# Attention scores taken from the longest block of queries to the shortest, weights normalised in pairs, and a head turned from its last keys to its first

## The chip, the cores and the metric

The kernel runs on one core of one Trainium2 chip. The metric is the device time of one execution in microseconds (us), as the median of several runs. TensorE (PE in the rows) multiplies matrices; VectorE (DVE), ScalarE (ACT) and GpSimd (POOL) work on tiles element by element; SyncE (SP) only issues transfers, and POOL issues some too.

## The reference, cut to what matters

Two layers stand behind each other, on 512 tokens of 1024 numbers. The change lies in layer 1, forgetting attention with 16 heads of 64:

```python
q, k, v, g, f = jnp.split(h @ w_in, [FOX_W, 2 * FOX_W, 3 * FOX_W, 4 * FOX_W], axis=-1)
q = _rms_norm(q.reshape(b, s, FOX_HEADS, FOX_HD), q_gain).transpose(0, 2, 1, 3) * (FOX_HD ** -0.5)
k = _rms_norm(k.reshape(b, s, FOX_HEADS, FOX_HD), k_gain).transpose(0, 2, 1, 3)
cum = jnp.cumsum(log_f, axis=1).transpose(0, 2, 1)
for qs in range(0, s, Q_BLOCK):                      # Q_BLOCK = 128: four blocks of queries
    qe = qs + Q_BLOCK
    logits = (jnp.einsum('bhqd,bhkd->bhqk', q[:, :, qs:qe], k[:, :, :qe])
              + cum[:, :, qs:qe, None] - cum[:, :, None, :qe])
    causal = jnp.arange(qs, qe)[:, None] >= jnp.arange(qe)[None, :]
    p = jax.nn.softmax(jnp.where(causal, logits, -jnp.inf), axis=-1)
    outs.append(jnp.einsum('bhqk,bhkd->bhqd', p, v[:, :, :qe]))
o = jnp.concatenate(outs, axis=2).transpose(0, 2, 1, 3).reshape(b, s, FOX_W)
return (o * jax.nn.silu(g)) @ w_out
```

Block `i` of queries sees `(i + 1) * 128` keys, so the four blocks of a head have 128, 256, 384 and 512 columns.

## The kernel before, in words

**Scheduling.** The program is recorded as tasks and then put in order, when it is built, by a list scheduler (`Sched.order`): a planner with its own costs keeps one queue for each engine and takes from it the ready task with the smallest due time (`prio`), if its buffers are free. The due time is the PE work recorded so far, less an offset. `merge` and `zip2` interleave generators, so that attention (the side) is due a little ahead of the projections (the main work). What comes out is one fixed order for each engine, and an engine that waits holds all that stands behind it. All instructions go through one helper, so the profile gives line 442 for nearly all of them, and they are told apart by their tiles.

**A head of attention.** `stacks(pair)` turns the normalised q and k of two heads (tile `qn`) and splits them into a high and a low part (`st`). `scores(head)` works on the four blocks: two matmuls into a PSUM bank `r` (`r<-st,st`, 128, 256, 384 or 512 columns), an addition of the bias `ck` with a running minimum on DVE (`lg<-r,ck`, the custom instruction, which also gives the row's minimum `mn`), and the exponential on ACT with its row sum (`lg<-lg,t` and a read of the accumulator). After the fourth block one reciprocal of the four sums (`t<-t`, 128x4) follows on DVE, and then POOL multiplies each block by its reciprocal (`TENSOR_SCALAR lg<-lg,t`), blocks 0, 1, 2, 3. `turn(head)` transposes the weights on PE (`r<-ident,lg`), for each block `j` of keys the blocks of queries `j` to 3, and splits the bank into a high part (ACT, `ph<-r`) and a low part (DVE, `ph<-r,ph`). `values(head)` multiplies them with v (`r<-ph,v`), `j` from 0 to 3, and adds the two halves into `oT`. In `heads`, `scores(h + 1)` runs interleaved with `turn(h)`, and then `values(h)` with `stacks` of a later pair.

**What runs beside it.** The projections of the second half of q, k, v (`p<-wh,big`, `p<-wl,big`) run beside heads 0 to 7, and those of the gate (`p<-big,wh`, `p<-big,wl`) beside heads 8 to 15. The rms norm of q and k is a chain of short DVE instructions on 128x16 tiles (`t<-t,t`, `t<-t`) that ends in two products `qn<-qn,t`. Weights come as `raw` and are split into `wh` (ACT) and `wl<-raw,wh` (DVE); the last ones are first multiplied by a gate (`raw<-raw,gate`, DVE). After the last exponential ACT takes the Silu of the gate (`qn<-qn`), DVE multiplies (`oT<-oT,qn`), both split it (`goh`), and the output projection (`a<-wh,goh`) starts.

**Buffers.** The blocks of one head lie in three buffers: blocks 0 and 2 share one, block 1 and block 3 have their own. There are four PSUM banks of kind `r`, shared by scores, turns, values and stacks.

Of the kernel before, what the change touches and what calls it, by code (L numbers as in the profile page):

```python
# [19 lines left out]
NT = S // P  # L20
# [501 lines left out]
def trunk(tc, x, c, positions, mod_w, mod_b, norm_g, ret_w_in, ret_w_out, fox_w_in, fox_b_f,  # L522
# [6 lines left out]
    with ExitStack() as es:  # L529
# [7 lines left out]
        V, A, G, T, SY = s.vector, s.scalar, s.gpsimd, s.tensor, s.sync  # L537
# [4 lines left out]
        def small(n=1):  # L542
            return s.buf("t", n)
# [4 lines left out]
        def pr_(n=512):  # L548
            return s.buf("r", n)
# [31 lines left out]
        def split(src, dst_h, dst_l, eng=None):  # L581
            A.copy(dst_h, src)
            (eng or V).tensor_tensor(out=dst_l, in0=src, in1=dst_h, op=ALU.subtract)
# [214 lines left out]
        for nm_ in ORD.split():  # L798
            if nm_[0] == "m":
                j, nj = int(nm_[1]), int(nm_[3])  # L800
# [354 lines left out]
        def blocks(kind, dt):  # L1155

            b = [s.buf(kind, 512, dt) for _ in range(5)]
            return [(b[0], b[1]), (b[2][:, 0:384], b[3][:, 0:384]), (b[4][:, 0:256], b[4][:, 256:512]),
                    (b[2][:, 384:512], b[3][:, 384:512])]
# [305 lines left out]
        stk, prob, ptr, last_exp = {}, {}, {}, [None]  # L1465

        def scores(head):

            q, k, kx = stk.pop(head)
            ck = s.buf("ck", 7 * P)  # L1470
            with s.at(-30.0):
                SY.dma_start(ck, cum_dram[head].partition_broadcast(P))
                G.dma_start(ck[:, 2 * P:3 * P], k_mask[:, 0:P], accum_op=ALU.add)
                G.dma_start(ck[:, 4 * P:7 * P], k_mask, accum_op=ALU.add)
            cks = [ck[:, 6 * P:], ck.rearrange("p (k n) -> p k n", k=7, n=P)[:, 0:6:5, :], ck[:, 0:3 * P],
                   ck[:, 0:6 * P].rearrange("p (k n) -> p k n", k=2, n=3 * P)[:, :, 0:2 * P]]
            b = [s.buf("lg") for _ in range(3)]
            lg = [b[0][:, 384:512], b[2][:, 0:256], b[0][:, 0:384], b[1]]
            mn, sm, rs = small(NT), small(NT), small(NT)
            for i in range(NT):  # L1480
                n = (i + 1) * P
                ps = pr_()
                cs = slice(i * P, n)
                T.matmul(ps[:, 0:n], q[:, cs], k[:, 0:n], start=True, stop=False)
                T.matmul(ps[:, 0:n], q[:, cs], kx[:, 0:n], start=False, stop=True)

                def two(v):
                    return v.rearrange("p (k n) -> p k n", k=2, n=n // 2) if i % 2 else v

                V.tensor_tensor_reduce(out=two(lg[i]), in0=two(ps[:, 0:n]), in1=cks[i], scale=1.0, scalar=3.0e38,  # L1490
                                       op0=ALU.add, op1=ALU.min, accum_out=mn[:, i:i + 1])
                last_exp[0] = A.activation(lg[i], lg[i], AF.Exp, bias=mn[:, i:i + 1], scale=-1.0,
                                           accum_out=sm[:, i:i + 1])
                if i == NT - 1:
                    V.reciprocal(rs, sm)
                    for j in range(NT):
                        G.tensor_scalar(out=lg[j], in0=lg[j], scalar1=rs[:, j:j + 1], scalar2=1.0,
                                        op0=ALU.mult, op1=ALU.mult)
                    prob[head] = lg
                yield max(2 * n, 512) / 512 * 0.216  # L1500

        def turn(head):

            parts = prob.pop(head)
            pt = ptr[head] = blocks("ph", F32R)
            for j in range(NT):
                w = S - j * P
                ps = pr_()
                for i in range(j, NT):
                    T.transpose(ps[:, (i - j) * P:(i - j + 1) * P], parts[i][:, j * P:(j + 1) * P], ident)  # L1510
                split(ps[:, 0:w], *pt[j])
                yield (NT - j) * 0.107
# [31 lines left out]
        def heads(lo, hi, nxt):  # L1544

            for h in range(lo, hi):
                if h + 1 < nxt:
                    yield from zip2(scores(h + 1), turn(h))
                else:
                    yield from turn(h)  # L1550
                if h % 2 == 1 and h // 2 + 2 < nxt // 2:
                    yield from zip2(stacks(h // 2 + 2), values(h))
                else:
                    yield from values(h)
# [33 lines left out]
        run(q0)  # L1588
        merge(proj1("k", 0), forget_gates(), 0.5, B1, s)
        merge(proj1("v", 0), chain(stacks(0), stacks(1), scores(0)), 0.3, B1, s)  # L1590
        merge(proj1("qkv", 1), heads(0, 8, 16), R1, B1, s)
        merge(chain(*[proj_g(j) for j in range(4)]), heads(8, 16, 16), R2, B1, s)
# [77 lines left out]
```

## Time and profile before

| | us |
|---|---|
| median of 3 runs | 731.32 |
| lowest, highest | 730.45, 733.33 |
| profiled execution, its own time | 731.09 |
| its span, first to last instruction | 729.3 |
| mean granted clock of TensorE, share of full speed | 0.992 |

The span is that of one execution, and its own time is 1.8 us above the span. Attention in layer 1 takes from about 480 us to 680 us of the span. Of a matmul the profile models the end, so a "busy" PE can hide a short wait; the spacing of two starts shows it. For DVE, ACT and POOL the row gives the duration, and in brackets the idle time ahead of the row and who ended it.

### The profile page before, as it was taken

To read this page: it belongs to the slowest core of one execution; us is meant where nothing else is said; L and a number is where in the kernel's file an instruction comes from. 1 tells how busy PE (TensorE), PEld (TensorE's weight loads), DVE (VectorE), ACT (ScalarE), POOL (GpSimd) and SP (SyncE) were. 2 spreads that over 40 slices of the span, in tenths; PEclk is the share of its full clock that TensorE was granted. 3 is DMA by queue.
4 is the path that set the end of the run, shared out by engine and by line. 5 is a ranking of instruction groups with operands and counts; after the bars stand their busy time and mean duration, and the time that the engine had idled before them with its cause. 6 is when DMAs were issued, how large, how long until landed. Compare 5 with 4: busy or idle time off the path is not lost.

```text
span 729.3 us, 10006 instructions
## 1 busy us (share of the span) xinstructions
PE 707.8 (97%) x3386; PEld 579.1 (79%) x3386; DVE 587.5 (81%) x1257; ACT 394.2 (54%) x733; POOL 118.9 (16%) x167
## 2 busy tenths in 40 slices
PE   7999999999999999999999999999999999998995
PEld 6777888888887888888888887787778688877884
DVE  5899999989996899899381869877688967788925
ACT  6558563654354435554150554447758566778613
POOL 1001100100110011000000100054343354444011
PEclk9999999999999999999999999999999999999998
DMA  8994764794757674625435127494545566667002
GB/s 281 348 310 95 176 210 131 201 269 135 174 142 200 192 172 140 175 91 200 131 121 185 74 75 256 145 233 112 152 106 138 147 152 152 130 156 260 1 11 104
DMA packets 78546, 118.25 MB, mean 162 GB/s; under 512 B 6952, under 2 KB 39840, under 8 KB 78496
## 3 DMA queue, kind: packets, MB, share of 16 engines
q1 hardware_dynamic: 66176, 98.71, 42.6%
q0 software_dynamic: 12320, 18.91, 14.7%
q8 instruction: 26, 0.43, 0.2%
q14 instruction: 24, 0.20, 0.1%
HBM read 109.16 MB, written 4.25 MB: 156 GB/s over the span
## 4 chain that ended last, share of the span: by engine, by line
PE 77%; DVE 10%; DMA 5%; issue 3%; ACT 2%; POOL 1%; SPq 1%; DVEq 0%; POOLq 0%; ACTq 0%
PE p L442 44%; PE a L442 18%; PE r L442 15%; DMA raw<-in_mod_w 4%; DVE wl L442 2%; DVE t L442 1%; DVE macc L442 1%; POOL lg L442 1%; DVE st L442 1%; DVE ph L442 1%; DVE sx L442 1%; SPq L442 1%; DVE tg L442 1%; DVE lg L442 1%; DMA raw<-in_fox_w_in 1%
## 5 line engine op out<-in xcount | busy, mean ns | idle before, releaser
L442 ACT CAST wh<-raw 128x1024 fp32r<-128x1024 f32 x120 | 124.8, 1052 | 80.9 <-PE p L442 40.8
L442 DVE TENSOR_TENSOR wl<-raw,wh 128x1024 fp32r<-128x1024 f32 x120 | 146.9, 1229 | 26.0 <-ACT wh L442 23.0
L442 PE MATMUL p<-wh,big 128*128 128x512 f32 x384 | 136.3, 403 | 0.0
L442 PEld LDWEIGHTS p<-wh,big 128*128 128x128 f32 x384 | 72.1, 189 | 13.3
L442 PE MATMUL p<-wh,sf 128*128 128x512 f32 x256 | 79.7, 390 | 0.0
L442 PE MATMUL p<-wl,big 128*128 128x512 f32 x192 | 76.8, 400 | 0.0
L442 PE MATMUL p<-wh,act 128*128 128x512 f32 x192 | 64.2, 396 | 1.2 <-DVE big L442 1.2
L442 POOL DMA_DIRECT2D raw<-in_ret_w_in x16 | 19.4, 1239 | 268.3 <-DVE raw L442 87.8
L442 DVE SCALAR_TENSOR_TENSOR macc<-raw,csilu,macc 128x512 f32<-128x512 f32 x80 | 59.7, 747 | 2.8 <-DMA raw<-in_mod_w 2.0
L442 PE MATMUL a<-wh,go 128*128 128x512 f32 x192 | 61.7, 392 | 0.0
L442 POOL TENSOR_SCALAR lg<-lg,t 128x128 f32<-128x128 f32 (+1 forms) x64 | 43.3, 759 | 80.0 <-DVE t L442 75.4
L442 PEld LDWEIGHTS p<-wh,sf 128*128 128x128 f32 x256 | 48.0, 188 | 10.3 <-ACT u L442 0.3
L442 PE MATMUL p<-act,wh 128*128 128x512 f32 x160 | 53.1, 393 | 0.0
L442 PE MATMUL p<-wl,sf 128*128 128x512 f32 x128 | 50.0, 391 | 0.0
L442 ACT ACTIVATE lg<-lg,t 128x128 f32<-128x128 f32 (+1 forms) x64 | 36.2, 566 | 19.3 <-DVE t L442 18.8
L442 PE MATMUL p<-big,wh 128*128 128x512 f32 x128 | 45.7, 415 | 0.0
L442 PEld LDWEIGHTS p<-wh,act 128*128 128x128 f32 x192 | 36.0, 188 | 8.4 <-issue 1.6
L442 PEld LDWEIGHTS a<-wh,go 128*128 128x128 f32 x192 | 36.0, 188 | 7.0
L442 PEld LDWEIGHTS p<-wl,big 128*128 128x128 f32 x192 | 36.2, 189 | 6.1
L442 PE MATMUL r<-act,sh 128*128 128x512 f32 x120 | 40.6, 391 | 0.0
L442 POOL DMA_DIRECT2D ck<-in_k_mask x32 | 28.6, 1047 | 69.2 <-DVE t L442 55.3
L442 PE MATMUL p<-wl,act 128*128 128x512 f32 x96 | 38.3, 398 | 0.6 <-DVE wl L442 0.6
(184 smaller groups left out, 1521.5 us busy)
## 6 DMA issues: line engine op xcount, KB each, us to landing
raw<-in_ret_w_in SPq DMA_DIRECT2D x48, 512.0 KB, 5.6
raw<-in_mod_w SPq DMA_DIRECT2D x64, 256.0 KB, 6.5
raw<-in_fox_w_in SPq DMA_DIRECT2D x32, 512.0 KB, 4.6
raw<-in_ret_w_in POOLq DMA_DIRECT2D x16, 512.0 KB, 8.8
raw<-in_mod_w SPq DMA_DIRECT2D x16, 512.0 KB, 4.6
raw<-in_ret_w_out SPq DMA_DIRECT2D x16, 512.0 KB, 4.2
ck<-cum_dram SPq DMA_DIRECT2D x16, 448.0 KB, 4.5
x<-in_x SPq DMA_DIRECT2D x16, 256.0 KB, 5.4
```

Source lines behind the costliest of these rows:

```text
L442: getattr(eng, op)(*[real(v) for v in args], **{k: real(v) for k, v in kw.items()})
```

## The change

The blocks of queries are taken from block 3 (512 columns) to block 0. A reciprocal is now taken for two blocks at a time, as soon as the second of the pair has its sum: for blocks 2 and 3, and then for blocks 1 and 0; POOL multiplies block 3, 2, 1, 0 in that order. `turn` goes from the last block of keys, which needs block 3 alone, to the first, which needs all four. `values` is unchanged and still begins with the first block of keys.

```diff
-            for i in range(NT):
+
+            for i in reversed(range(NT)):
                 n = (i + 1) * P
                 ps = pr_()
                 cs = slice(i * P, n)
@@
                 last_exp[0] = A.activation(lg[i], lg[i], AF.Exp, bias=mn[:, i:i + 1], scale=-1.0,
                                            accum_out=sm[:, i:i + 1])
-                if i == NT - 1:
-                    V.reciprocal(rs, sm)
-                    for j in range(NT):
+                if i % 2 == 0:
+                    V.reciprocal(rs[:, i:i + 2], sm[:, i:i + 2])
+                    for j in (i + 1, i):
                         G.tensor_scalar(out=lg[j], in0=lg[j], scalar1=rs[:, j:j + 1], scalar2=1.0,
                                         op0=ALU.mult, op1=ALU.mult)
-                    prob[head] = lg
+                prob[head] = lg
                 yield max(2 * n, 512) / 512 * 0.216
 
         def turn(head):
 
             parts = prob.pop(head)
             pt = ptr[head] = blocks("ph", F32R)
-            for j in range(NT):
+            for j in reversed(range(NT)):
                 w = S - j * P
                 ps = pr_()
                 for i in range(j, NT):
```

The planner's order moves with it from head 0 on. Three places show how.

**PE, the transposes of the last head (15).** Before: `lg_6637` holds blocks 0 and 2, `lg_6657` block 1, `lg_6694` block 3; the banks `r_6738`, `r_6755`, `r_6767`, `r_6780` take the blocks of keys 0 to 3.

```order
L442 MATMUL r_6738<-ident,lg_6637 128x128
L442 MATMUL r_6755<-ident,lg_6637 128x128
L442 MATMUL r_6767<-ident,lg_6637 128x128
L442 MATMUL p_6736<-big_3872,wh_6328 128x512
L442 MATMUL p_6736<-big_3880,wh_6328 128x512
L442 MATMUL p_6736<-big_3872,wl_6343 128x512
L442 MATMUL r_6738<-ident,lg_6694 128x128
L442 MATMUL r_6755<-ident,lg_6694 128x128
L442 MATMUL r_6767<-ident,lg_6694 128x128
L442 MATMUL r_6780<-ident,lg_6694 128x128
```

After, on PE at the same place: `lg_6638` is block 3, `lg_6658` holds blocks 2 and 0, `lg_6678` is block 1; `r_6728`, `r_6732`, `r_6741` take the blocks of keys 3, 2 and 1, and `r_6763`, four rows further on, block 0.

```order
L442 MATMUL r_6728<-ident,lg_6638 128x128
L442 MATMUL p_6548<-big_3889,wh_6274 128x512
L442 MATMUL r_6732<-ident,lg_6658 128x128
L442 MATMUL r_6732<-ident,lg_6638 128x128
L442 MATMUL p_6548<-big_3903,wh_6274 128x512
L442 MATMUL p_6548<-big_3889,wl_6287 128x512
L442 MATMUL r_6741<-ident,lg_6678 128x128
L442 MATMUL r_6741<-ident,lg_6658 128x128
L442 MATMUL r_6741<-ident,lg_6638 128x128
```

Before, the transposes follow the blocks of queries as they come, into up to four open banks, and all four that read block 3 stand at the end; after, a bank is filled in one go, and the first need only the block that is normalised first.

**PE, from the last turn but one to its values (head 14).** Before: the last transpose into the bank of key block 0 (`r_6648`), and the first matmul of the values (`r_6712<-ph_6696`), which reads it.

```order
L442 MATMUL r_6648<-ident,lg_6598 128x128
L442 MATMUL r_6664<-ident,lg_6598 128x128
L442 MATMUL r_6678<-ident,lg_6598 128x128
L442 MATMUL p_6670<-big_3872,wl_6343 128x512
L442 MATMUL p_6670<-big_3872,wh_6328 128x512
L442 MATMUL p_6670<-big_3880,wh_6328 128x512
L442 MATMUL p_6670<-big_3872,wl_6343 128x512
L442 MATMUL r_6700<-ident,lg_6598 128x128
L442 MATMUL p_6670<-big_3872,wh_6328 128x512
L442 MATMUL p_6670<-big_3880,wh_6328 128x512
L442 MATMUL p_6670<-big_3872,wl_6343 128x512
L442 MATMUL r_6712<-ph_6696,v_5865 128x512
```

After, on PE from the same transpose (now into `r_6689`) to the two matmuls that read the high part (`ph_6701`) and the low part (`ph_6708`) of key block 0:

```order
L442 MATMUL r_6689<-ident,lg_6550 128x128
L442 MATMUL p_6548<-big_3889,wl_6287 128x512
L442 MATMUL p_6548<-big_3889,wh_6274 128x512
L442 MATMUL p_6548<-big_3903,wh_6274 128x512
L442 MATMUL p_6548<-big_3889,wl_6287 128x512
L442 MATMUL r_6710<-ph_6701,v_5886 128x512
L442 MATMUL p_6548<-big_3889,wh_6274 128x512
L442 MATMUL p_6548<-big_3903,wh_6274 128x512
L442 MATMUL p_6548<-big_3889,wl_6287 128x512
L442 MATMUL r_6710<-ph_6708,v_5886 128x512
```

Seven 512-column matmuls and three transposes stood between the bank and the first matmul that reads it; now four matmuls stand there.

**DVE, the last rms norm of k.** Before: the chain on `t_5596` and `t_5599`, with the reciprocal of one head (`t_5601`) in it.

```order
L442 TENSOR_SCALAR t_5596<-t_5583 128x16
L442 TENSOR_TENSOR t_5599<-t_5596 128x16
L442 RECIPROCAL t_5601<-t_5490 128x4
L442 TENSOR_TENSOR t_5599<-t_5599,t_5583 128x16
L442 SCALAR_TENSOR_TENSOR t_5596<-t_5599,t_5596 128x16
L442 TENSOR_TENSOR t_5599<-t_5596 128x16
```

After, on DVE: the same chain is on `t_5614` and `t_5617`, and the last reciprocal ahead of it (`t_5534`) belongs to that head's blocks 1 and 0.

```order
L442 RECIPROCAL t_5534<-t_5495 128x2
L442 SCALAR_TENSOR_TENSOR t_5518<-t_5525,t_5518 128x16
L442 TENSOR_TENSOR qn_5451<-qn_5451,t_5518 128x512
L442 TENSOR_TENSOR qn_5477<-qn_5477,t_5518 128x512
L442 TENSOR_REDUCE t_5550<-tm_5563 128x8
L442 TENSOR_TENSOR ph_5596<-r_5539,ph_5572 128x512
L442 TENSOR_SCALAR t_5603<-t_5550 128x16
L442 TENSOR_TENSOR wl_5605<-raw_5461,wh_5579 128x1024
L442 TENSOR_SCALAR t_5614<-t_5603 128x16
L442 TENSOR_TENSOR t_5617<-t_5614 128x16
L442 TENSOR_TENSOR t_5617<-t_5617,t_5603 128x16
```

The reciprocals have moved out of the last chain into the one before it.

## Rows read from the trace of the kernel before

**Rows 1.** The page's first part: busy time of each engine, its share of the span, and its instructions.

```profile
PE 707.8 (97%) x3386; PEld 579.1 (79%) x3386; DVE 587.5 (81%) x1257; ACT 394.2 (54%) x733; POOL 118.9 (16%) x167
```

**Rows 2.** Busy time by stretch: the stretch in us from the span's start and its length, then busy us (and instructions) of PE, PEld, DVE, ACT, POOL, the granted clock, the DMA share and GB/s. The first is all of attention, the others are 20 us each in it.

```profile
480.00:680.00 200.00, 194.40 (x1012) 157.99 (x1011) 155.04 (x374) 140.35 (x317) 79.74 (x122) 1.00 0.61 150
520.00:540.00 20.00, 19.70 (x101) 15.70 (x101) 19.48 (x58) 16.41 (x38) 4.84 (x8) 1.00 0.54 132
560.00:580.00 20.00, 18.27 (x95) 14.10 (x94) 19.06 (x53) 12.03 (x27) 5.92 (x10) 1.00 0.58 146
640.00:660.00 20.00, 18.75 (x104) 15.49 (x103) 17.04 (x42) 14.17 (x35) 8.21 (x12) 1.00 0.54 133
660.00:680.00 20.00, 18.02 (x90) 14.56 (x89) 17.61 (x32) 17.36 (x34) 5.38 (x4) 1.00 0.67 235
```

**Rows 3.** Who waited for whom from 480 to 680 us, PE and its weight load (PEld): waiting engine and tile, releaser, then us in total, times, longest.

```profile
PE r L442 <- POOL lg L442: 3.3, 4, 1.8
PE r L442 <- DVE qn L442: 1.5, 1, 1.5
PEld r L442 <- POOL lg L442: 5.0, 5, 2.3
```

**Rows 4.** The timeline of PE at six places: start, us, instruction, and in brackets the idle time ahead of it. The last two rows are an undisturbed pair, the two before them an undisturbed run of four transposes and what follows.

```profile
496.46 0.40 PE L442 MATMUL p<-wl,big 128*128 128x512 f32 x1
497.13 0.33 PE L442 MATMUL r<-ident,lg 128*128 128x128 f32 x1 [0.27 <-POOL lg L442]
...
535.82 0.39 PE L442 MATMUL p<-wh,big 128*128 128x512 f32 x1
536.45 0.33 PE L442 MATMUL r<-ident,lg 128*128 128x128 f32 x1 [0.24 <-DVE ph L442]
...
571.32 0.40 PE L442 MATMUL p<-wl,big 128*128 128x512 f32 x1
573.23 0.33 PE L442 MATMUL r<-ident,qn 128*128 128x128 f32 x1 [1.52 <-DVE qn L442]
...
649.74 0.39 PE L442 MATMUL p<-big,wh 128*128 128x512 f32 x1
651.18 0.33 PE L442 MATMUL r<-ident,lg 128*128 128x128 f32 x1 [1.06 <-POOL lg L442]
...
664.42 0.44 PE L442 MATMUL p<-big,wh 128*128 128x512 f32 x1
665.02 0.33 PE L442 MATMUL r<-ident,lg 128*128 128x128 f32 x1 [0.16 <-POOL lg L442]
...
667.36 0.40 PE L442 MATMUL p<-big,wl 128*128 128x512 f32 x1
669.58 0.66 PE L442 MATMUL r<-ident,lg 128*128 128x128 f32 x4 [1.82 <-POOL lg L442]
669.99 0.71 PE L442 MATMUL p<-big,wh 128*128 128x512 f32 x2
...
677.32 0.39 PE L442 MATMUL p<-big,wl 128*128 128x512 f32 x1
677.55 0.39 PE L442 MATMUL a<-wh,goh 128*128 128x512 f32 x1
```

**Rows 5.** The timeline of POOL: the four normalisations of one head merged into a row (x4, all four widths), at three heads, and the widest block of the last head alone.

```profile
541.66 2.05 POOL L442 TENSOR_SCALAR lg<-lg,t 128x128 f32<-128x128 f32 x4 [8.00 <-DVE t L442]
...
569.42 2.37 POOL L442 TENSOR_SCALAR lg<-lg,t 128x128 f32<-128x128 f32 x4
...
664.14 5.38 POOL L442 TENSOR_SCALAR lg<-lg,t 128x128 f32<-128x128 f32 x4 [4.64 <-DVE ph L442]
...
666.39 3.13 POOL L442 TENSOR_SCALAR lg<-lg,t 128x512 f32<-128x512 f32 x1
```

**Rows 6.** The timeline of DVE at two of these places: at 570 us an instruction of the rms norm and the same one 2.3 us later, and at 666 us the products of the output stage.

```profile
569.95 1.87 DVE L442 SCALAR_TENSOR_TENSOR t<-t,t 128x16 f32<-128x16 f32 x1
...
572.27 0.18 DVE L442 SCALAR_TENSOR_TENSOR t<-t,t 128x16 f32<-128x16 f32 x1
...
666.48 1.27 DVE L442 TENSOR_TENSOR oT<-oT,qn 128x512 f32<-128x512 f32 x2
667.68 0.68 DVE L442 TENSOR_TENSOR goh<-oT,goh 128x512 fp32r<-128x512 f32 x1
668.29 0.67 DVE L442 TENSOR_TENSOR oT<-oT,qn 128x512 f32<-128x512 f32 x1
```

**Rows 7.** Groups by shape from 480 to 680 us: instruction, count | busy us, mean ns of one | idle us before, releasers.

```profile
L442 DVE CUSTOM_DVE_ANT_0 lg<-r,ck 128x128 f32<-128x128 f32 x16 | 4.5, 284 | 7.1 <-PE r L442 7.0
L442 DVE RECIPROCAL t<-t 128x4 f32<-128x4 f32 x16 | 2.8, 172 | 2.2 <-ACT lg L442 2.2
...
L442 ACT ACTIVATION_READ_ACCUMULATOR lg<-lg,t 128x1 f32 x64 | 12.3, 192 | 0.0
L442 ACT ACTIVATE lg<-lg,t 128x128 f32<-128x128 f32 x16 | 6.5, 403 | 5.4 <-DVE t L442 5.1
```

**Rows 8.** The timeline of ACT and of DVE behind the four transposes at 669.58 us: the high and the low part of a bank of 512 columns.

```profile
669.94 0.59 ACT L442 CAST ph<-r 128x512 fp32r<-128x512 f32 x1 [2.15 <-PE r L442]
...
670.56 0.69 DVE L442 TENSOR_TENSOR ph<-r,ph 128x512 fp32r<-128x512 f32 x1 [1.60 <-ACT ph L442]
```

## The prediction, made before the changed kernel was run

> **What bounds the kernel now.** I read the busy times first: PE is busy for 97% of the span [rows 1]. The change removes no matmul and adds none (3386 before; the built order holds as many after), so it can only take away time in which PE waits, or add some. Then the stretches [rows 2]: in attention, 480 to 680 us, PE is busy 194.40 of 200 us, so 5.6 us are idle in plain sight, most of them at 560 to 580 and 640 to 680. The list of waits names the releasers [rows 3]: POOL's normalised weights (`lg`), for the matmuls and still more for the weight loads, and once the normalised q and k (`qn`). Since a busy PE can hide a short wait, I measured the stops by the spacing of starts in the timeline [rows 4]: undisturbed, a matmul of 512 columns is followed after 0.23 us (677.32 to 677.55) and a transpose after 0.10 (669.58 to 669.99 for four). What goes beyond 0.23 is the stop:
> at 496.46: 0.67 − 0.23 = 0.44; at 535.82: 0.63 − 0.23 = 0.40; at 649.74: 1.44 − 0.23 = 1.21; at 664.42: 0.60 − 0.23 = 0.37; at 667.36: 2.22 − 0.23 = 1.99. These five end at a transpose of weights and sum to **4.41 us**. The sixth, at 571.32, ends at a transpose of q or k: 1.91 − 0.23 = **1.68 us**. Together 6.09 us, 0.83% of the time: no more than about that can be won, while what can be lost has no such bound.
>
> **Why they arise.** The four normalisations of a head take 2.05 us on POOL when nothing disturbs them, and 5.38 us at the last head; there the block of 512 columns alone takes 3.13 us [rows 5], beside four DVE products that read two tiles of SBUF each and follow each other without a gap [rows 6]. Block 3 is last in POOL's queue, and by the order four transposes of the last head stand together behind it. At 569 us it is the other way round: POOL's four take 2.37 us, and in that time a DVE instruction on 16 columns takes 1.87 us where its like takes 0.18 [rows 5, 6]. It is a link in the rms norm of k, whose end (`qn`) PE awaits at 573.23.
>
> **Part a: scores from long to short, pairs, turn from the last keys.** In the new order the first transposes of a head need block 3 alone, which now is first in POOL's queue, and the last pair is only 384 columns wide. The tightest place I find in the order is the last head: between its last score matmul (128 columns) and the first transpose that needs the pair 1 and 0 stand 14 matmuls of 512 columns, seven transposes and six narrow matmuls, 14 × 0.23 + 7 × 0.10 + about 0.7 = 4.6 us of PE work. What must fit in there: DVE 0.28, ACT 0.40 + 0.19, reciprocal 0.17 [rows 7] and POOL's block 1, under 0.6 (four widths take 2.05, rows 5), so 1.6 us if nothing stands ahead. By the order the split of a bank stands ahead, its high part on ACT (0.59) and its low part on DVE (0.69) [rows 8]: 2.9. Then two products of the gate stand right behind the reciprocal on DVE, and if they hold POOL as in [rows 6] that is 1.3 more, 4.2, and with two products of the output behind them 5.5. So 0 to 0.9 us of the 3.57 at the end of attention (1.21 + 0.37 + 1.99) remain; I take 0.5, and 0.1 for the two earlier places, where the distance in the order is larger. Part a: 4.41 − 0.6 = **−3.8 us**. At worst, half of it stays (−2.2).
>
> **Part b: the stop behind the rms norm.** The reciprocal that let POOL start at 569.42 stood inside the last chain; in the new order both reciprocals of that head stand ahead of it, with a split of weights between, so POOL should be done. The pairs still meet the chain before (both reciprocals stand in that one), and DVE there is full: 19.06 of 20 us at 560 to 580 [rows 2]. The bounds are 0 (it waits as long, elsewhere) and −1.68; nearer the second by the order, **−1.2 us**.
>
> The Trainium skill (SBUF — State Buffer, "Who interferes with whom") says that a DVE instruction with two SBUF inputs contends with a GpSimd instruction that reads SBUF, and that whichever starts first holds the shared ports for its whole instruction. The trace agrees that the two block each other, but not in who wins: at 666.39 POOL's row starts ahead of DVE's at 666.48, and POOL is the one held [rows 5, 6]; and at 569.95 DVE waits 1.87 us, longer than any single block, through the rest of a run of four. By the rule a run of two would cost DVE as much as a run of four, one instruction, and part b would be 0; by the rows it shrinks with the run.
>
> **Part c: 16 more reciprocals.** There are 32 instead of 16; the trace shows none of 128x2, and the one of 128x4 takes 0.17 us [rows 7], so 2.75 us of DVE at most. DVE is busy 155 of 200 us [rows 2], and its idle time covers most of it. Where that cover is gone, at 520 to 540 and 560 to 580 (19.48 and 19.06 of 20), 1.6 additional ones fall in each 20 us, 3 × 0.17 = 0.5 us at most on the path to PE. Between 0 and 0.5 I take **+0.3**.
>
> **Part d: values right behind the last turn.** `values` begins with key block 0. Before, that was turned first; now it is turned last, as the widest bank, and its split stands directly between the transposes and the values. What that needs: ACT starts 0.36 us after the first of four transposes (669.58 to 669.94), DVE ends at 671.25, 1.67 after it [rows 4, 8], that is about 1.3 after the last transpose (1.67 less three times 0.10). What the new order gives it at head 14: eight matmuls of 512 columns, 8 × 0.23 = 1.84 us to the matmul that reads the low part. So 0.5 us to spare if both engines are free; but a short exponential (0.40 + 0.19) can stand ahead on ACT and a reciprocal (0.17) on DVE, and then it is 2.1 against 1.84. Bounds: 0, and 0.3 for each of 16 heads, 4.8. Most heads have more room in the order than head 14; nearer the first, 0.06 per head: **+1.0 us**.
>
> ACT and POOL do the same work as before, and no transfer is added or removed; the bias transfers on POOL's queue now stand between the two pairs of some heads. The trace shows POOL idle for most of a head (8.00 us ahead of one run, rows 5), which hides them.
>
> **Sum.** −3.8 − 1.2 + 0.3 + 1.0 = −3.7 us. The profiled execution took 731.09 us (span 729.3 and 1.8 around it), 0.2 below the median 731.32, so I forecast 731.09 − 3.7 = **727.4 us**. A measurement of this kernel tells about 0.5%, 3.7 us, from no change; the forecast lies just beyond that, so near the bound that the chances must say the rest.
>
> **The rivals.**
> *The waits stay, with other neighbours.* PE's order is fixed by a planner that knows nothing of POOL and DVE holding each other; a new order brings meetings of its own. For it: the rows show the holding at three separate places. Against it: the distances grew nearly everywhere. Half of part a and nothing of b: −2.2 + 0.3 + 1.0, 730.2 us.
> *POOL and DVE hold each other by the instruction, not by the run.* Then b is 0: −3.8 + 0.3 + 1.0, 728.6 us. This is what the page's rule named above would give here. The 1.87 us row speaks against it.
> *Slower: every head waits for its widest bank.* The place is the first two matmuls of `values`. If ACT and DVE run behind the planner there by more than the room, each head stops PE. The gains above, less the reciprocals, are 4.7 us, so it decides from 4.7 / 16 = 0.29 us per head on, and it is slower by over 0.5% (735.0) from (3.9 + 4.7) / 16 = 0.54. With 0.5 per head: −3.8 − 1.2 + 0.3 + 8.0, 734.4 us. For it: room is only 1.84 to about 4.4 us in the new order where it was 2.2 to 10. Against it: gate matmuls stand in between at every head, and DVE has a fifth of its time free.
> *All of it goes and nothing comes:* 731.09 − 6.1 = 725.0 us. The projections still fill PE to the end of attention.
>
> **How the numbers follow.** Forecast (725.8 to 729) 0.50; waits stay (729 to 732) 0.24; by the instruction (728 to 729) 0.08; slower for the values (732 to 737) 0.10; all goes (724.5 to 725.8) 0.08. The forecast's own range is 725.8 to 729. The range 724.8 to 731.8 leaves out most of the slower case and little else, under 2 in 10. Faster by over 0.5% is below 727.7: all of the last case and some seven tenths of the forecast, 0.44. Slower by over 0.5%, above 735.0: most of the slower rival and what I can't see, 0.09. The rest, 0.47, is the same.
>
> **What the new profile would show.** Part a: PE's list of waits without `POOL lg` but for some tenths, PE busy over 197 of 200 us in attention, and no stop above 0.9 us between the last head's scores and its values; wrong if `POOL lg` still holds 2 us or more. Part b: no stop above 0.5 us ahead of a transpose of `qn`, though a 16-column DVE instruction of the earlier chain may still be stretched. Part c: 32 reciprocals of at most 0.17 us. Part d: new waits of PE for `ACT ph` or `DVE ph` of about 1 us in all; the forecast is wrong if they reach 4. It would also be wrong if the output projection started late after attention; before, it followed without a gap at 677.55.

## The result, and the profile after

The change makes the kernel faster: 725.64 us in the median of six runs (724.80 to 727.37) against 731.12 of six runs of the kernel before beside them, a ratio of 0.9926 (95% interval 0.9911 to 0.9942), 5.5 us. The forecast was 727.4 with a range of 724.8 to 731.8: side and range held, the gain was named 1.8 us too small.

The profiled execution took 727.05 us, its span 725.3. First the busy times on its page, to be read beside [rows 1]:

```profile
PE 706.3 (97%) x3386; PEld 579.3 (80%) x3386; DVE 586.7 (81%) x1273; ACT 394.1 (54%) x733; POOL 118.6 (16%) x167
```

No matmul more or less; DVE has 16 instructions more. Then the stretches, to be read beside [rows 2] (columns as there):

```profile
480.00:680.00 200.00, 198.06 (x1037) 162.93 (x1036) 159.69 (x399) 143.43 (x322) 80.74 (x124) 1.00 0.60 153
540.00:560.00 20.00, 19.34 (x101) 15.83 (x100) 13.02 (x28) 11.88 (x25) 9.43 (x14) 1.00 0.68 175
560.00:580.00 20.00, 19.04 (x96) 14.35 (x94) 18.87 (x54) 12.75 (x28) 6.88 (x10) 1.00 0.50 124
640.00:660.00 20.00, 20.00 (x117) 16.90 (x116) 18.08 (x50) 16.91 (x42) 8.69 (x12) 1.00 0.35 102
660.00:680.00 20.00, 20.00 (x96) 16.47 (x95) 19.49 (x31) 15.79 (x29) 0.00 (x0) 1.00 0.67 214
```

PE is busy for 198.06 of 200 us where it was 194.40, and the stretch from 640 to 680 us, which had 3.23 us of idle time (20 − 18.75 and 20 − 18.02), has none; its last 6.5 us are now the output. From 660 us on POOL does nothing any more: the normalisations that stood there are done earlier. The list of waits for 480 to 680 us, beside [rows 3], PE's matmuls:

```profile
PE r L442 <- DVE st L442: 1.2, 2, 0.7
PE r L442 <- DVE qn L442: 0.4, 1, 0.4
PE r L442 <- ACT ph L442: 0.3, 1, 0.3
```

and for the weight loads, three of six rows:

```profile
...
PEld r L442 <- ACT ph L442: 2.0, 6, 0.7
PEld r L442 <- DVE qn L442: 1.3, 3, 0.8
PEld r L442 <- DVE ph L442: 0.6, 3, 0.3
...
```

`POOL lg`, 3.3 us for the matmuls and 5.0 for the weight loads before, is gone from both. Of the single stops, the largest that is left, the one ahead of `qn`, and the end of attention, in PE's timeline (beside [rows 4]):

```profile
547.92 0.40 PE L442 MATMUL p<-wh,big 128*128 128x512 f32 x1
548.98 0.41 PE L442 MATMUL r<-ident,lg 128*128 128x128 f32 x2 [0.66 <-DVE st L442]
...
566.47 0.39 PE L442 MATMUL p<-wh,big 128*128 128x512 f32 x1
567.27 0.33 PE L442 MATMUL r<-ident,qn 128*128 128x128 f32 x1 [0.41 <-DVE qn L442]
...
673.28 0.39 PE L442 MATMUL p<-big,wl 128*128 128x512 f32 x1
673.51 0.39 PE L442 MATMUL a<-wh,goh 128*128 128x512 f32 x1
```

The first is 1.06 − 0.23 = 0.83 us, and its releaser is a DVE instruction on `st`, not POOL; the stop ahead of `qn` is 0.80 − 0.23 = 0.57 us where it was 1.68. The output follows attention without a gap at 673.51, 4.04 us earlier than the 677.55 of [rows 4], although in this profiled execution attention began 1.67 us later (its first score matmul stands at 484.76 against 483.09). So of the two profiled executions the changed one is shorter by 731.09 − 727.05 = 4.04 us: 5.71 us less in attention, below, and 1.67 us more ahead of it.

**Attention as a sum.** I took the spacing of each two starts on PE, less the usual spacing behind the same kind of matmul in the same trace, for all of attention, from the first score matmul to the first matmul of the output, and counted what is above 0.15 us by the kind of matmul that came late. That is the reading of [rows 4], done for every matmul. The profiled executions of the kernels of this study, without e5 and e11, which lose their cover (below):

| kernel | attention | weights | qn | scores | values | stops | attention less stops | median time |
|---|---|---|---|---|---|---|---|---|
| before | 194.46 | 5.17 | 1.69 | 1.05 | 0.42 | 8.33 | 186.13 | 730.8 to 731.2 |
| changed | 188.75 | 2.15 | 0.57 | 0.00 | 0.73 | 3.44 | 185.30 | 725.64 |
| e1 turn only | 191.79* | 3.38 | 0 | 1.07 | 1.70 | 6.15 | 185.65 | 729.52 |
| e2 turn forward | 188.96 | 2.09 | 0 | 0.37 | 0.67 | 3.12 | 185.84 | 725.33 |
| e3 no pairs | 190.29 | 2.65 | 0.78 | 0 | 1.67 | 5.09 | 185.19 | 726.40 |
| e4 pairs only | 188.45 | 1.47 | 0 | 0.27 | 1.08 | 2.82 | 185.64 | 725.74 |
| c1 | 193.32 | 2.66 | 1.67 | 0.77 | 2.24 | 7.34 | 185.98 | 729.75 |
| c2 | 189.35 | 1.37 | 0.56 | 0 | 1.73 | 3.65 | 185.69 | 725.34 |
| e6 | 189.53 | 1.54 | 0 | 0.31 | 1.63 | 3.48 | 186.05 | 725.76 |
| e8 | 191.65 | 3.14 | 0 | 0.68 | 1.68 | 5.50 | 186.15 | 727.86 |
| e9 | 190.71 | 2.28 | 0 | 0.66 | 1.68 | 4.62 | 186.09 | 727.39 |
| e10 | 192.05 | 2.18 | 0 | 3.09 | 0.45 | 5.72 | 186.33 | 728.21 |

(*e1 does part of the last head's values after its first output matmul; its output is 1.07 us longer.) The column that counts is "attention less stops": 185.2 to 186.3 in all twelve. To 1.1 us attention costs the same PE work in each, and the kernels differ by the sum of their stops. The output (43.29 us from its first to its last start) and what follows that last start (8.45 before, 8.46 after) did not move.

The same stops can be sorted by what ended them in the trace (to about 0.1 us). Those that end with POOL's `lg` sum to 4.01 us before and 1.69 in c1, to 3.09 in e1, 1.75 in e8, 1.42 in e10, 1.24 in e2, 0.86 in e9, 0.36 in e4 and 0.17 in e3; in the changed kernel, c2 and e6 there are none. What is left without these and without those at `qn` lies between 1.9 and 4.3 us and shows no trend with the change: 2.6 before, 2.9 in the changed kernel, 4.0 in c1.

### The profile page after: what moved, and what is told of

The parts are those of the page before. It is cut to its first block, busy times and chain, and to the rows that moved or that the text cites. A ratio compares the mean times of both kernels' runs of the same rounds, so it can differ in the third digit from the quotient of the medians.

```text
span 725.3 us, 10079 instructions
## 1 busy us (share of the span) xinstructions
PE 706.3 (97%) x3386; PEld 579.3 (80%) x3386; DVE 586.7 (81%) x1273; ACT 394.1 (54%) x733; POOL 118.6 (16%) x167
## 4 chain that ended last, share of the span: by engine, by line
PE 82%; DMA 7%; DVE 5%; ACT 3%; issue 2%; POOL 1%; SPq 0%; DVEq 0%; ACTq 0%; POOLq 0%
PE p L442 46%; PE a L442 18%; PE r L442 16%; DMA raw<-in_mod_w 3%; DMA tg<-in_positions 1%; PE s L442 1%; DMA ck<-in_k_mask 1%; DVE macc L442 1%; DVE t L442 1%; POOL lg L442 1%; ACT st L442 1%; DVE st L442 1%; ACT lg L442 1%; ACT wh L442 1%; DMA x<-in_x 1%
## 5 line engine op out<-in xcount | busy, mean ns | idle before, releaser
L442 POOL TENSOR_SCALAR lg<-lg,t 128x512 f32<-128x512 f32 (+1 forms) x64 | 42.6, 714 | 83.0 <-DVE t L442 68.9
L442 ACT ACTIVATE lg<-lg,t 128x512 f32<-128x512 f32 (+1 forms) x64 | 35.9, 563 | 9.2 <-DVE t L442 8.7
L442 PE MATMUL a<-wl,go 128*128 128x512 f32 x96 | 37.7, 393 | 0.0
```

What stands on the lines that cost most here:

```text
L442: getattr(eng, op)(*[real(v) for v in args], **{k: real(v) for k, v in kw.items()})
```

## The experiments

The theory: the gain is the stops that end at transposes of weights and at `qn`, and they come from POOL being late and held by DVE. The rivals: a new order has other meetings by luck; or one part of the change does all of it. Ratios are to the kernel before on the same chip.

**Which part does it: e1 to e4.** e1 is the kernel before with one line of the change:

```diff
-            for j in range(NT):
+            for j in reversed(range(NT)):      # turn
```

> The kernel before with the turn alone reversed (scores from block 0, one reciprocal of four). My theory, the distance theory: the gain comes from the distance between POOL's last normalisation and the first transposes that need it. Here the first transpose needs block 3, which POOL normalises last, so no distance is won and the values stand closer behind the turn: 731 to 735 us, stops at weights' transposes of 4 us or more in all. Rival, the turn theory (the gain comes from one open bank at a time instead of four): about 727 us.

Measured: 729.52, ratio 0.9981 [0.9971, 0.9991]. The turn from the last keys alone gives 1.4 us, no more than another order of the same kernel gives by itself (c1, below), so it can't be put down to the turn. POOL still takes the 512 columns last, and these are now needed first; PE's list of waits from 480 to 680 us still names POOL:

```profile
PE r L442 <- POOL lg L442: 2.4, 3, 1.4
```

e2 is the changed kernel with that line put back:

```diff
-            for j in reversed(range(NT)):
+            for j in range(NT):                # turn
```

> The changed kernel with the turn put back to the first keys first; scores from the longest block and pairs stay. Distance theory: the last pair is short, so POOL is done sooner and most of the gain stays, 726 to 729 us, and the stop of 2 us at the end of attention is gone. Turn theory: the gain is gone, about 731 us.

Measured: 725.33, 0.9926 [0.9911, 0.9941], as the changed kernel. The reversal of the turn isn't needed. e3 is the changed kernel with one reciprocal behind the last block:

```diff
-                if i % 2 == 0:
-                    V.reciprocal(rs[:, i:i + 2], sm[:, i:i + 2])
-                    for j in (i + 1, i):
+                if i == 0:
+                    V.reciprocal(rs, sm)
+                    for j in reversed(range(NT)):
```

> The changed kernel with one reciprocal of all four sums after block 0, POOL in the order 3, 2, 1, 0; turn reversed. Distance theory: block 3 is still normalised first and needed first, so half to most of the gain stays, 726 to 729 us; what the pairs bring, POOL's earlier start, is under 2 us. If the pairs are what matters (they shorten POOL's runs, which hold DVE): 730 to 731 us, and a DVE instruction of 16 columns stretched beyond 1.5 us.

Measured: 726.40, 0.9937 [0.9922, 0.9952]: most of the gain without the pairs. e4 is the kernel before with the pairs alone, scores and turn as they were:

```diff
-                if i == NT - 1:
-                    V.reciprocal(rs, sm)
-                    for j in range(NT):
+                if i % 2:
+                    V.reciprocal(rs[:, i - 1:i + 1], sm[:, i - 1:i + 1])
+                    for j in (i - 1, i):
...
-                    prob[head] = lg
+                prob[head] = lg
```

> The kernel before with pairs alone: reciprocals for blocks 0 and 1, then 2 and 3; scores from block 0, turn from the first keys. Distance theory: the second pair is the wide one and is still awaited by four transposes, a little is won (POOL has 1.3 us of work left instead of 2.05): 729 to 731 us. Pairs theory: about 727 us.

Measured: 725.74, 0.9929 [0.9914, 0.9944]: the whole gain by an edit of four lines. POOL's rows of the last head show how:

```profile
655.08 0.83 POOL L442 TENSOR_SCALAR lg<-lg,t 128x128 f32<-128x128 f32 x2 [2.86 <-DVE t L442]
658.35 1.25 POOL L442 TENSOR_SCALAR lg<-lg,t 128x384 f32<-128x384 f32 x2 [2.45 <-PE r L442]
```

The first pair is done 2.4 us before the second begins, and both together take 2.08 us, as undisturbed, where the run of four took 5.38 [rows 5]. So the pairs alone get POOL out of the way, because less is left to do behind the last sum. Without the pairs, reversed scores with POOL's order and the turn reversed too (e3) do nearly as much; the reversed scores by themselves (e10, below) do half.

**Is it luck: c1, c2.** A constant of the planner that the change doesn't touch (what it adds for a signal between engines) is moved a little, in the kernel before (c1) and in the changed one (c2); that gives each another order.

```diff
-    LAT = 0.2
+    LAT = 0.21
```

> The kernel before, but the planner counts 0.21 instead of 0.20 us for a signal between engines: the same edit nowhere in attention, another fixed order of the same instructions. It is a control for luck. If the stops of before belong to how scores, POOL and turn are chained (distance theory): 729 to 732.5 us, with a stop of 1 us or more at the weights' transposes at the end of attention. If the order of before merely fell badly (luck theory): 725 to 728 us.

> The changed kernel with the same control, 0.21 instead of 0.20 us in the planner. Distance theory: 724.5 to 727.5 us, no stop above 1 us in attention. Luck theory: anything from 724 to 731.

Measured: c1 729.75, 0.9985 [0.9973, 0.9996]; c2 725.34, 0.9917 [0.9900, 0.9934]. Another order moves the time by 1.5 us in the kernel before and by under 1 us in the changed one, and leaves 4.4 us (729.75 − 725.34) between them, so most of the gain isn't the luck of one order; about 1 us of it may be. But the table warns: in c1 the stops at weights are half of before's (2.66) and those at values five times (2.24). The sum stands, its split into kinds doesn't. Head 13's stop of 1.21 us is gone in c1, and the last head's 0.37 + 1.99 have become 0.71 + 0.54, though POOL works as before; `qn` keeps its 1.67.

**Would telling the planner do: e5, e6.** The planner's price of POOL's normalisation is doubled per column, in the kernel before (e5) and in the changed one (e6), so that it places the transposes later.

```diff
-            return 0.1 + n / (510.0 if op == "tensor_scalar" else 450.0)
+            return 0.1 + n / (255.0 if op == "tensor_scalar" else 450.0)
```

> The kernel before, but the planner counts twice as much per column for POOL's normalisations (2.0 instead of 1.0 us for 512 columns), as they take when DVE holds them; it then puts the transposes later. Distance theory: the stops go without any edit in attention, 726 to 728.5 us, the last stop of 2 us under 0.7. If the order within a head matters by itself: 730 us or more.

> The changed kernel with the same dear normalisations in the planner. Distance theory: hardly a stop at POOL's weights is left to take away, so 724.5 to 727 us, within 0.2% of the changed kernel. If POOL still costs PE something unseen there: 723 to 724.

Measured: e5 740.81, 1.0129 [1.0107, 1.0152], a plain miss; e6 725.76, 0.9927 [0.9913, 0.9942]. In e5 no matmul of the gate is left behind the last score matmul (46 were before, 60 in the changed kernel): they all stand earlier, and PE waits with nothing in between for the last head's chain (PE's waits from 480 to 690 us):

```profile
PE r L442 <- POOL lg L442: 3.4, 5, 1.7
PE r L442 <- ACT ph L442: 2.3, 1, 2.3
PE r L442 <- DVE t L442: 2.0, 2, 1.8
```

Attention takes 200.48 us, 6.0 more than before, and the output 48.53, 5.2 more; in the 20 us from 680 us on the mean granted clock was 0.76, so a part of them was at the lower of its two levels (1.2 and 2.4 GHz). So this price is no cure, but with the cover gone the run doesn't tell whether later transposes alone would be. e6 shows that with the change the price hardly matters.

**POOL out of the way: e8, e9.** In the kernel before, the normalisation of some heads goes to ACT, for head 6 alone (e8) or for heads 6, 13 and 15 (e9), whose POOL rows stand ahead of the stops of 1.68, 1.21 and 0.37 + 1.99 us.

```diff
                     for j in range(NT):
+                        if head in (6,):          # e9: (6, 13, 15)
+                            A.activation(lg[j], lg[j], AF.Copy, scale=rs[:, j:j + 1])
+                            continue
```

> The kernel before, with the normalisation of one head alone (head 6, whose four POOL rows stand at 569.42 to 571.79 beside the stretched link of the rms norm) put on ACT. Theory (POOL's run of four holds DVE's 16-column instruction, and through it PE's stop of 1.68 us at 571.3): the 1.87 us row falls to under 0.4 and the stop at the transpose of q or k falls below 0.6, so the time falls by 1.1 to 1.7, to 729.3 to 729.9. Rival (the chain of the rms norm is late by the amount of DVE's own work, and POOL is beside the point): the stop stays above 1.2 and the time stays at 730.5 to 731.3.

Measured: 727.86, 0.9962 [0.9947, 0.9977]. At the place in question DVE's timeline reads:

```profile
569.33 0.18 DVE L442 SCALAR_TENSOR_TENSOR t<-t,t 128x16 f32<-128x16 f32 x1
569.54 1.29 DVE L442 TENSOR_TENSOR qn<-qn,t 128x512 f32<-128x512 f32 x2
```

and PE's:

```profile
570.60 0.27 PE L442 MATMUL r<-ident,qn 128*128 128x128 f32 x1
570.62 0.71 PE L442 MATMUL p<-wh,big 128*128 128x512 f32 x2
```

The link that took 1.87 us [rows 6] takes 0.18, and the transpose of `qn` starts without a wait. So POOL's run of four did hold DVE's chain, and that was PE's stop. The time fell by 2.9 us, more than that stop; the rest is the new order behind head 6 (weights 5.17 to 3.14, values 0.42 to 1.68 in the table), and the smallest fall that the interval admits (1.7 us) is that of the stop alone. In that order head 13's stop of 1.21 us is gone, and of the last head's 2.36 us 1.3 are left (0.98 and 0.31), though POOL still normalises both heads. PE's timeline at the last head:

```profile
661.69 0.40 PE L442 MATMUL p<-big,wh 128*128 128x512 f32 x1
662.90 0.33 PE L442 MATMUL r<-ident,lg 128*128 128x128 f32 x1 [0.81 <-POOL lg L442]
...
663.98 0.40 PE L442 MATMUL p<-big,wl 128*128 128x512 f32 x1
664.52 0.33 PE L442 MATMUL r<-ident,lg 128*128 128x128 f32 x1 [0.15 <-POOL lg L442]
```

> The kernel before, with the normalisation of three heads (6, 13 and 15, whose POOL rows stand ahead of the stops of 1.68, 1.21, and 0.37 + 1.99 us) put on ACT; the order of blocks, the one reciprocal and the turn stay. Theory (these stops come from POOL's late and held normalisations, and the change won by getting POOL out of the way): nearly all of the 5.25 us goes, and the time is 725.8 to 727.2, close to the changed kernel's. Rival (the last head's weights are late by their place in the order, whoever normalises them, and only an earlier start helps): the stops in the last 20 us of attention stay above 2 us together, and the time is 728.5 to 730.5.

Measured: 727.39, 0.9957 [0.9943, 0.9971]. The stretches:

```profile
480.00:680.00 200.00, 197.89 (x1029) 161.46 (x1028) 154.39 (x377) 145.67 (x330) 68.31 (x109) 1.00 0.59 149
...
660.00:680.00 20.00, 20.00 (x100) 16.51 (x99) 17.51 (x32) 18.60 (x36) 0.00 (x0) 1.00 0.62 214
```

PE's waits from 480 to 680 us:

```profile
PE r L442 <- DVE ph L442: 0.8, 3, 0.3
PE r L442 <- DVE st L442: 0.6, 1, 0.6
PE r L442 <- POOL lg L442: 0.5, 2, 0.3
```

From 660 us on PE is without idle time as in the changed kernel, with neither reversal nor pairs. The clean comparison is with e8, whose stops are nearly the same up to 645 us: there the last head's transposes waited for POOL, and here, with ACT, they don't wait, so the rival "late by their place, whoever normalises" falls for the last head. A stop of 0.42 us behind head 14's POOL comes in its place; attention is 0.9 us shorter than in e8, and the two times (727.35 to 728.59 and 726.87 to 727.89) overlap. For head 13 nothing is shown, as its stop was gone in e8 already. The 3.4 us won are three fifths of the change's gain and 0.2 above the range I gave: the stops at values and those of the 13 other heads remain.

**Order of scores, order on POOL: e10, e11.** e10 takes of the change only the reversed scores (one reciprocal, POOL's order and the turn as before):

```diff
-            for i in range(NT):
+            for i in reversed(range(NT)):
...
-                if i == NT - 1:
+                if i == 0:
```

> Of the change only the reversal of the scores: the longest block first, one reciprocal behind the shortest, POOL's normalisations in the order of before (128, 256, 384, 512 columns) and the turn from the first keys. Theory (what counts is when the last weight of a head is ready against the first transpose; a short last block shortens the chain ahead of POOL by 0.69 less 0.28 us on DVE and some tenths on ACT, but the block of 512 columns, last on POOL, still has the longest way): half to two thirds of the gain, 727 to 728.5. Rival (any order of the scores with new neighbours does it): within 0.5 us of the changed kernel, 725.2 to 726.2. Second rival (only a start in pairs helps): 729.5 to 731.

Measured: 728.21, 0.9958 [0.9942, 0.9974], within what I gave, but only in part for the reason that I gave: stops at weights fall as far as in the changed kernel (2.18), 1.42 of them still released by POOL, and most of what is lost is at the scores (3.09). e11 is the kernel before with POOL's order reversed and nothing else:

```diff
-                    for j in range(NT):
+                    for j in reversed(range(NT)):   # POOL's normalisations
```

> The kernel before with POOL's four normalisations of a head in the order 512, 384, 256, 128 columns behind the same one reciprocal; nothing else is edited. Theory (what counts is how long before its first transpose the whole of a head's weights is done; the run of four is as long as before, and with the turn from the first keys the first transposes need the 128 columns, now last): no gain, 730 to 732, with stops at weights of 3 us or more in attention. Rival (the block of 512 columns being last is itself the cause): those stops fall below 1.5 us and the time is 727.5 to 729.

Measured: 743.62, 1.0167 [1.0134, 1.0200]. No gain, as expected, but 12 us slower, which I had not expected: attention takes 205.76 us, 11.3 more than before, and the output 45.69, 2.4 more. Again no gate matmul is left behind the last score matmul, and the longest single wait stands behind one row of POOL's timeline:

```profile
681.09 4.62 POOL L442 TENSOR_SCALAR lg<-lg,t 128x384 f32<-128x384 f32 x1
```

Beside it DVE's timeline:

```profile
680.54 1.10 DVE L442 TENSOR_TENSOR raw<-raw,gate 128x512 f32<-128x512 f32 x1
681.57 1.88 DVE L442 TENSOR_TENSOR oT<-oT,qn 128x512 f32<-128x512 f32 x3
683.38 0.67 DVE L442 TENSOR_TENSOR goh<-oT,goh 128x512 fp32r<-128x512 f32 x1
683.98 0.67 DVE L442 TENSOR_TENSOR oT<-oT,qn 128x512 f32<-128x512 f32 x1
684.58 0.68 DVE L442 TENSOR_TENSOR goh<-oT,goh 128x512 fp32r<-128x512 f32 x1
```

PE's timeline:

```profile
676.83 1.71 PE L442 MATMUL r<-ph,v 128*128 128x512 f32 x8
686.57 2.39 PE L442 MATMUL r<-ident,lg 128*128 128x128 f32 x10 [8.02 <-POOL lg L442]
688.61 0.77 PE L442 MATMUL a<-wh,goh 128*128 128x512 f32 x1
```

and PE's waits from 480 to 700 us:

```profile
PE r L442 <- POOL lg L442: 12.6, 4, 8.0
```

A normalisation of 384 columns stays on POOL for 4.62 us, to 685.71, just past the end of the last of six back-to-back products on DVE (685.26), and PE waits 8 us, until POOL's four are done. Why the planner spends its gate matmuls earlier in e5 and e11 I didn't try.

## Why the prediction was right, and where it fell short

**Part a, the stops at weights (−3.8).** Right in kind: no stop of the new profile is put down to POOL, and the five named places (4.41 us) are gone. One of the five was not POOL's: the row of 536.45 names DVE's `ph` [rows 4], and POOL's last normalisation had ended 4.5 us before, so POOL's share was 4.01. By the table weights fell from 5.17 to 2.15, −3.0; what is left is behind DVE's `st` (the 0.83 above, the largest) or too short to be named a wait; the estimate of 0.6 us left had no place for that. The cause I gave is shown for the last head by e9 against e8. For head 13 it stays argued: before, POOL's row of 2.48 us at 648.65 ends as the transposes begin, but e8 and c1 lose that stop by their order alone. The stop behind `ph` is still there in e9 (0.46).

**Part b, the stop behind the rms norm (−1.2).** 1.69 to 0.57, −1.1. The pairs do meet the chain, as feared, but briefly. POOL's first pair in its timeline:

```profile
563.51 1.26 POOL L442 TENSOR_SCALAR lg<-lg,t 128x512 f32<-128x512 f32 x2 [7.50 <-DVE t L442]
```

and DVE's links beside it:

```profile
563.37 0.18 DVE L442 TENSOR_TENSOR t<-t 128x16 f32<-128x16 f32 x1
563.58 0.64 DVE L442 TENSOR_TENSOR t<-t,t 128x16 f32<-128x16 f32 x1
564.25 0.54 DVE L442 SCALAR_TENSOR_TENSOR t<-t,t 128x16 f32<-128x16 f32 x1
```

Two links are stretched, each to the end of one POOL instruction of the pair, together 0.8 us more than twice 0.17; the first product of `qn` takes 0.94 us beside the second pair, the next one 0.68. The Trainium skill (SBUF — State Buffer, "Who interferes with whom") calls the shared ports an exclusive lock and says, of DVE's two-port modes, that whoever issues first has them "for the whole instruction". The two links agree with a hold by the instruction; the row of 1.87, longer than any of POOL's four beside it, does not, and no run settles why. The rival that rested on the rule, with no gain in part b, fell all the same: the stretches beside the pairs (0.8 us, and 0.3 at the product) are less than the 1.7 us (1.87 − 0.17) of the one beside the run of four. For POOL the rule does not hold in e11: one instruction that had started ahead of three `oT` products, with a product on `raw` under way, waited through all of them. That POOL held the chain in the order of before is shown by e8; the meeting itself belongs to that order and to c1's, for in e1 and e10 the stop at `qn` is gone though POOL still has its run of four.

**Part c, the reciprocals (+0.3).** The group of the 32 new ones from 480 to 680 us:

```profile
L442 DVE RECIPROCAL t<-t 128x2 f32<-128x2 f32 x32 | 5.1, 159 | 3.1 <-ACT lg L442 3.0
```

5.1 us instead of 2.8 [rows 7]. No wait of PE points to them, and e3, which has 16 as before, is not faster (726.40) than the changed kernel, so no cost of them can be seen.

**Part d, values right behind the last turn (+1.0).** Stops at values went from 0.42 to 0.73, e2 has 0.67 with the turn from the first keys, and c1 shows 2.24 without any of the change, so by the runs it costs nothing that can be told from another order. The rival that made it decide (734.4) had no support.

**What was missing.** The terms came to −3.7; attention fell by 194.46 − 188.75 = 5.71: −3.0 at weights, −1.1 at `qn`, −1.05 at scores, +0.3 at values, and −0.8 in spacings each under 0.15 us. The step that failed is the list it began from: I took six stops for all that could be won ("6.09 us … no more than about that"), where there were 15 above 0.15 us with 8.33 us together, the scores' among them, and I set 1.3 us of costs (c and d) against it, of which at most 0.3 came. Weights gave 0.8 less than named, and scores and small spacings 1.9 that were not in the sum, so that the total came as near as it did is partly luck; what ends the small spacings stays open. So the result, 725.64, lies 0.2 us inside the case "all of it goes" (724.5 to 725.8), to which I gave 0.08, and not in the forecast's own range, 725.8 to 729; of the sum, c and d had to be zero and the small stops had to count. And one reason was tied to the wrong line: the prediction bound the gain to the turn from the last keys, and e2 and e4 have it all without that. Of the signs named ahead, PE above 197 us (198.06), no `POOL lg`, 32 short reciprocals and no gap at the output came; the stop ahead of `qn` is 0.57 instead of below 0.5.

## What to carry to other kernels

Where PE is nearly always busy, sum the excess of every spacing of its starts over the usual one, not only the stops that the list of waits names: here attention less that sum is the same within 1.2 us in twelve kernels. Give an engine that another one can hold its work in pieces as soon as each is ready; the same work in one run behind the last sum can lie on the path. And look at how much independent work the order leaves behind the last chain: two small edits after which none was left there cost 10 to 13 us, more than the whole change won, though that this alone is the cause was not tried.

## What was not expected of the hardware

POOL's `TENSOR_SCALAR` of 384 columns took 4.62 us in e11 beside six uninterrupted DVE products from SBUF, where its like took 0.58 us at 670.32 in the same trace, and 512 columns took 3.13 us in [rows 5]. In both cases POOL's row ends 0.45 to 0.56 us after the last product of DVE's run (685.26, and 668.96 in [rows 6]), so here the hold was as long as the run. In the same kernel, in the stretches in which PE waited (14.43 and 13.43 of 20 us busy), the mean granted clock was 0.91 and then 0.74, so a part of each was at the lower of the two levels, 1.2 and 2.4 GHz. The ten transposes behind the wait of 8.02 us take (688.61 − 686.57) / 10 = 0.20 us each, where an undisturbed one takes 0.10 [rows 4]. The two stretches of e11 (columns as in [rows 2]):

```profile
660.00:680.00 20.00, 14.43 (x73) 11.84 (x71) 16.47 (x39) 13.85 (x33) 7.96 (x8) 0.91 0.37 113
680.00:700.00 20.00, 13.43 (x58) 11.56 (x59) 16.15 (x28) 13.41 (x26) 6.51 (x4) 0.74 0.24 71
```
